# Hybrid decoder trunk: when transposing transfers are issued, how their data are taken over, and one head that turns its values on PE

## The chip, the cores and the metric

One core of one Trainium2 chip. The metric is device time in microseconds (us): the time of one execution, here the median of three runs. Besides the timed runs one execution was profiled; its trace gives the start and length of each instruction on the engines PE (TensorE), ACT (ScalarE), DVE (VectorE), POOL (GpSimd) and SP (SyncE, which issues most transfers).

## The reference

512 tokens of width 1024 get 16 learned meta tokens put ahead of them (528 in all), pass two layers and a final norm, and the meta tokens are dropped. Everything is float32.

```python
h = concat([meta, x])                        # 528 x 1024
h = h + gla_branch(rmsnorm(h), ...)          # 4 heads, value width 512 each
h = h + diff_branch(rmsnorm(h), ...)         # 8 heads, value width 256 each
out = rmsnorm(h[16:], g_final)
```

The first layer is gated linear attention: per head it projects queries, keys, values and a gate, weighs score blocks of 128 x 128 tokens with a decay, multiplies them with the values, norms each row over the head's width, multiplies with the gate and projects back. The second layer is differential softmax attention: per head two score matrices of 528 x 528 with a position bias, `a = softmax1 - lam * softmax2`, `a @ v`, the same norm, gate and projection back.

## The kernel before, in words

**Precision.** Each float32 operand of a product is split into a high and a low part (`split`, L259: ACT copies to the high part, DVE subtracts to get the low one), and a product is three matmuls (high x high, high x low, low x high). So each weight block that comes in costs one ACT and one DVE instruction before PE can use it.

**Projections.** A projection of 256 output columns is a `Unit` (L384): seven products of 12 matmuls (`product`, L376) on sums and differences of the operand blocks. Its results come out in two planes of 128 channels x 528 tokens; when a plane is done, `tail(1)` (L442) and at the very end `tail(0)` (L461) are called. ACT moves partial results (L400), DVE adds them (L425, L427).

**Values must be turned.** Projections give channels on the partitions, and the value product needs tokens there. In the first head of each layer and in the very last head PE turns them: `to_tokens` (L796) makes four transposes of 128 x 128 (L801) and a short one for the meta tokens (L802) into two small banks, and `split` and `split3` (L350) take them over. `post` does this 2.4 us of filler after the plane is complete (L830). All other heads turn by transfers (`turn_by_dma`, L528): ACT copies a plane into two planes of 16-bit halves (L539) and writes them to DRAM (`vd`, L540); SP's transposing transfers bring them back with tokens on the partitions (L548, and the short `lands` for the meta tokens, L550); then `landed` (L521) takes the whole 128 x 1024 block over: ACT scales it to the high part by a constant `tick` (L523), DVE makes the low part (L525), and `split3` makes `vm`, the meta tokens' values (L355, L356, L360). `tick` is a small DVE memset (L554) tied behind the latest DVE addition (`W.mark`), so that ACT cannot take the block over before that place in DVE's order.

**Order of the work.** PE's instructions stay in program order. Those of ACT, DVE and SP are put in an order ahead of time, by program order as priority and by what is expected to be ready; functions marked `urgent` (L251) go 100 places ahead. During the run each engine works its list off in that order and waits in front of an instruction whose inputs are not there. Transposing transfers of L548 are kept in program order on SP.

Filler work (units, output projections) is a queue of generators in a `Weaver` (L74). `fill(us)` runs the next ones for so many us by their own count (a product counts 0.33 for three matmuls); the steps of a head (scores, value products, rows) are called between fills. `defer` and `follow` are clocks that run on this count: after both planes of a value unit have left, `follow` starts the transfers 8.0 us later and the takeover 10.0 us after that (L543). `W.land()` forces what is still out: in the first layer ahead of the blocks of a head (L1250), in the second at the start of a head (L1712).

**Weights.** `Weights` (L151) has a list of jobs and keeps two of them loaded (`fetch`, L166): when all parts of a job are split, it is dropped and the next but one is asked for, by `load` (L282), 1 MB into one of two `raw` buffers. A job enters the list when its unit is queued. In the second layer a head's queue is [output product of the pair before, in heads 2, 4 and 6], gate unit, value unit of the next head, key unit, query projection (L1716 to L1728; head 6 has another order); the next head's jobs enter only at that head's start (L1707).

**The second layer's steps.** L1738: A (scores), B (turn), C (values, `L348` on `v` and then L1587 on `vm`), E (rows) on blocks 3 to 0; step 4 of the list is C on block 3, the head's first value product. The filler is shared out by weights 1.5, 1.1, 1.1, 0.5 (L1741) with 3.0 us ahead of the first (L1744) and 3.0 held back (22.0 in head 6). The queue's length by its own count is 37.6 us a head (8.9 + 9.2 + 9.2 + 10.3), 60 with an output product (22.4).

**The first layer's heads.** From the value unit of head 1 on: values, output projection of the head before (heads 1 and 2 only), two gate units, landing, then the blocks (`gla_blocks`, L1140), whose first needs `vm` (L1152). In the last head the output projection of the head before comes after the landing, as the blocks' filler (L902 and L910).

Of the kernel before, what the change touches and what calls it, by code (L numbers as in the profile page):

```python
# [11 lines left out]
F32 = mybir.dt.float32  # L12
# [8 lines left out]
P = 128  # L21
# [52 lines left out]
class Weaver:  # L74


    def __init__(self):
        self.queue, self.late, self.left, self.stop = deque(), [], 0.0, None
        self.away = []

    def add(self, gen, us=0.0):
        self.queue.append(gen)
# [23 lines left out]

    def land(self):

        while self.away:
            self.onward(1000.0)  # L110

    def spent(self, us):
        self.onward(us)
# [37 lines left out]
class Weights:  # L151
# [44 lines left out]
    def done(self, p):  # L196
        self.room[p.kind] += 1
        self.pump()
# [8 lines left out]
def trunk(ctx, tc, x, meta, g_norm, gla_w_in, gla_w_gate_up, gla_b_gate, gla_gnorm, gla_w_out,  # L207
# [21 lines left out]
    def T(p, shape, dt, tag, **kw):  # L229
        uid[0] += 1  # L230
        return p.tile(shape, dt, tag=tag, name=f"{tag}_{uid[0]}", **kw)
# [36 lines left out]
    def load_w(w, r0, nk, c0):  # L268
        ncol = 2048 // nk
        t = T(wp, [P, nk, ncol], F32, "raw")  # L270
        sp.dma_start(t, w[r0:r0 + nk * P, c0:c0 + ncol].rearrange("(k p) c -> p k c", p=P))
        return t

    def load_blocks(w, c0):

        t = T(wp, [P, 4, 512], F32, "raw")
        for i in range(2):
            sp.dma_start(t[:, 2 * i:2 * i + 2, :].rearrange("p j (k c) -> p (j k) c", k=4),
                         w[:, c0 + i * P:c0 + (i + 1) * P].rearrange("(k p) c -> p k c", p=P))
        return t  # L280

    def load(key):  # L282
        return load_w(*key) if len(key) == 4 else load_blocks(*key)

    def w_pair(shape):
        return [T(wp, shape, F32R, tag) for tag in ("wh", "wl")]
# [4 lines left out]
        split(wh, wl, raw[:, :, ca:ca + ncol])  # L291
        return wh, wl

    W = Weaver()
    ws = Weights(lambda *key: load(key), {"pair": 2, "sum": 1, "a11": 1, "a12": 1, "a22": 1})

    def halves_of(c):
# [52 lines left out]
    def split3(dst, src, lo, scale=None):  # L350


        kw = {} if scale is None else {"scale": scale}
        hi = dst[:32].bitcast(F32)
        act.activation(dst[:32], src, AF.Copy, **kw)  # L355
        act.activation(dst[96 - lo:128 - lo], src, AF.Copy, **kw)  # L356
        if scale is None:
            dve.tensor_tensor(dst[lo:lo + 32], src, hi, op=ALU.subtract)
        else:
            dve.scalar_tensor_tensor(dst[lo:lo + 32], src, scale, hi, op0=ALU.mult, op1=ALU.subtract)  # L360
# [156 lines left out]
    def words(t):  # L517

        return t.bitcast(U16)

    def landed(hi, lo, src, one, rest):  # L521

        a = act.activation(hi, src, AF.Copy, scale=one)  # L523
        with tc.issue_after(a.ins):
            dve.tensor_tensor(lo, src, hi.bitcast(F32), op=ALU.subtract)  # L525
            rest()

    def turn_by_dma(planes, groups, ends, us, done):  # L528

        n = planes.shape[2]  # L530
        vd = T(dp, [2, P, 2, n], U16, "vd", bufs=3)
        rows = vd.rearrange("m p h c -> (m p h) c")
        raw = planes.rearrange("p m c -> p (m c)")[:, :2 * NR].rearrange("p (b c) -> p b c", c=2 * P)
        left, lands = [0, 1], []

        @urgent
        def leave(m, src):
            pl = words(planes[:, m, :]).rearrange("p (h c) -> p h c", h=2)
            act.activation(pl, words(src).rearrange("p (c h) -> p h c", h=2), AF.Copy)  # L539
            act.dma_start(vd[m], pl)  # L540
            left.remove(m)
            if not left:
                W.follow((8.0, turn), (us, land))  # L543

        def turn():
            for blocks, c0 in groups:
                o = words(raw[:, blocks, :])
                tc.keep_in_program_order(sp.dma_start(o, rows[:, c0:c0 + P * o.shape[1]], transpose=True))  # L548
            lands.append(T(mp, [P, 1, 2 * P], F32, "lands"))
            sp.dma_start(words(lands[0]), rows[:, ends:ends + P], transpose=True)  # L550

        def land():
            tick = T(mp, [P, 1], F32, "tick", bufs=2)
            tc.add_manual_dep(dve.memset(tick, 1.0).ins, W.mark.ins.name, mybir.DependencyInfo(  # L554
                mybir.DependencyClass.NoSync, mybir.DependencyReason.DATA), reason="place")
            done(raw, lands[0][:32, 0, :], tick)

        return leave

# [261 lines left out]
    def q_gla_v(hd, s):  # L821
        us = [want_unit(g_w_in, 2048 + 512 * hd + c) for c in (0, 256)] if hd else v_first

        def turned_back(m, vt):
            def post():
                pt, pm = to_tokens(vt, BLK, vt[:, :32])
                cs = slice(m * P, (m + 1) * P)
                split(s.v[0][:, :, cs], s.v[1][:, :, cs], pt.rearrange("p (b c) -> p b c", b=4))
                split3(s.vm[:, cs], pm, 32, short[:, NM:NM + 1])
            W.defer(2.4, post)  # L830

        def turner(h):
            def done(pt, pm, one):
                cs = slice(256 * h, 256 * h + 256)
                landed(s.v[0][:, :, cs], s.v[1][:, :, cs], pt, one, lambda: split3(s.vm[:, cs], pm, 32, short[:, NM:NM + 1]))
            return turn_by_dma(b_all[:, 2 * h:2 * h + 2, :], [(slice(0, 4), NM)], 0, 10.0, done)

        gens = []
        for h, u in enumerate(us):
            vts = []  # L840

            def dst(h=h, vts=vts):
                if h == 0:
                    s.vm = T(gp, [M3, 512], F32R, "vm0")
                    s.v = [T(gp, [P, 4, 512], F32R, f"v{i}") for i in range(2)]
                vts.extend([tmp(), tmp()])
                return vts

            if hd:
                gens.append(W.add(Unit(u, X, 1.0, dst, lambda i, vts=vts, leave=turner(h): leave(i, vts[i]))))  # L850
            else:
                def evac(i, banks, h=h, vts=vts, dst=dst):
                    if i == 0:
                        dst()
                    for n, bank in enumerate(banks):
                        act.activation(vts[i][:, n * HT:(n + 1) * HT], bank[:, :HT], AF.Copy)
                    turned_back(2 * h + i, vts[i])

                gens.append(W.add(plain_unit(u, evac)))
        return gens[0]  # L860
# [593 lines left out]
    def turned_back2(s, m, vt, first=False):  # L1454
        if not first:

            urgent(dve.tensor_copy)(vt[:, HT:HT + 8], vt[:, 2 * HT:2 * HT + 8])

        @urgent
        def post():  # L1460
            end = L if first else 272
            pt, pm = to_tokens(vt, RBLK if first else HBLK, vt[:, end - 32:end])
            cs = slice(m * P, (m + 1) * P)
            split3(s.vm[:, cs], pm, 32, short[:, NM + 1:NM + 2])
            split(s.v[0][:, :, cs], s.v[1][:, :, cs], pt.rearrange("p (b c) -> p b c", b=4))

        def done(pt, pm, one):
            landed(s.v[0], s.v[1], pt, one, lambda: split3(s.vm, pm, 32, short[:, NM + 1:NM + 2]))

        if first or s is heads[-1]:  # L1470
            W.defer(2.2 if first else 1.4, post)
        else:
            if m:
                s.leave = turn_by_dma(T(ep, [P, 2, 536], F32, "planes", bufs=1),
                                      [(slice(3, 1, -1), 0), (slice(1, None, -1), 272)], 240, 10.0, done)
            s.leave(m, vt[:, :536])

    def q_diff_z(hd, s):
# [228 lines left out]
    for hd in range(D_HEADS):  # L1707
# [1 line left out]
        s = heads[hd]  # L1709
        W.finish(projs[hd])  # L1710
        W.settle()
        W.land()  # L1712
        s.scored = False
        out2 = None
        keep = {D_HEADS - 1: 0.0, D_HEADS - 2: 22.0}.get(hd, 3.0)
# [29 lines left out]
        for n, (f, b) in enumerate(steps):  # L1745
            if last and n == 4:
                if values[hd] in W.queue:
                    W.finish(values[hd])
                W.settle()
                W.fill(2.0)  # L1750
            if n == 5 and gates[hd] in W.queue:
                W.finish(gates[hd])
            if last and n == 5:
                gfin = T(xp, [P, D], F32, "x0", bufs=1)
                sp.dma_start(gfin, g_final.partition_broadcast(P))
            if n == 5:
                if out2 in W.queue:
                    W.finish(out2)
                ys.append([yt[:, hd % 2, i] for i in range(2)])
            f(b)  # L1760
            if f is A and b == 0:
                s.scored, W.stop = True, None
                if not last:
                    heads[hd + 1].T = bias_tile(hd + 1)
            W.fill(max((W.left - keep) * share[f] / sum(share[g] for g, _ in steps[n:]),
                       (4.0 if hd % 2 == 0 else 3.0) if n == len(steps) - 2 else 2.4 if f is C else 0.0))
# [56 lines left out]
```

## Time and profile before

| | |
|---|---|
| median of 3 runs | 1008.28 us (1008.08 to 1010.28) |
| the profiled execution | 1010.31 us |
| its span, first to last instruction | 1008.5 us |
| PE's mean granted clock | 0.99 of full |
| value planes written for turning | 24 (12 from `keep`, first layer; 12 from `planes`, second) |
| transposing issues on SP | 30 (6 `keep`, 12 `planes`, 12 `lands`) |
| weight loads of the second layer on SP | 42 halves of 512 KB, landing after 5.5 us (median) |

Rows of a timeline are: start us, length us, engine, line, operation, output <- input, tile, count, and in brackets the engine's idle time before it and what ended it. An engine name with q (SPq, ACTq) is that engine's issue of a transfer, not the transfer. Rows with a count are merged, and their length runs from the first to the end of the last. Rows of stages are: from:to, length, busy time (and count) of PE, PEld (weight loads into the array), DVE, ACT, POOL, then PE's granted clock, the share in which the DMA engines were busy, and GB/s. Groups of a tile have least/median/greatest length in ns. Rows of waits have the total, the number and the longest, in us.

### The profile page before, as it was taken

How to read it: one execution, taken by the hardware profiler on the slowest of the kernel's cores; microseconds unless marked ns; L12 is line 12 of the kernel's file. 1: busy time of each engine (PE TensorE's matmuls, PEld its weight loads, DVE VectorE, ACT ScalarE, POOL GpSimd, SP SyncE). 2: the span in 40 equal slices, each digit the busy share in tenths (PEclk: the TensorE clock that was granted, in tenths of full speed). 3: DMA queues.
4: the chain of work that ended last, by engine and by line, in shares of the span. 5: the costliest groups of instructions: out<-in, count | busy, mean ns of one | idle time of the engine just before them, and what ended most of it. 6: DMA issues, size and time to landing. Idle time of an engine off the chain costs nothing. (4 is left out here: it accounts for less than half of the span.)

```text
span 1008.5 us, 18098 instructions
## 1 busy us (share of the span) xinstructions
PE 975.0 (97%) x7023; PEld 916.6 (91%) x7023; DVE 778.7 (77%) x1574; ACT 614.6 (61%) x1292; POOL 51.5 (5%) x68
## 2 busy tenths in 40 slices
PE   8999999999999999899999899999999999999997
PEld 7999999899999999799899799898998999988896
DVE  7888885877778787456998696886967879676785
ACT  6775855475546666536667476466774666654584
POOL 1000000001000100000000101001010010100001
PEclk8999999999999999899999999999999999999999
DMA  7212324541363336122232424335251362623212
GB/s 192 81 50 79 88 84 134 100 114 44 111 152 84 84 105 152 50 84 80 86 97 72 114 84 142 84 96 132 58 169 45 98 153 61 160 65 95 84 64 83
DMA packets 156296, 98.63 MB, mean 98 GB/s; under 512 B 38429, under 2 KB 142141, under 8 KB 156208
## 3 DMA queue, kind: packets, MB, share of 16 engines
q1 hardware_dynamic: 152752, 90.92, 33.7%
q10 hardware_dynamic: 3456, 6.54, 1.9%
q8 instruction: 55, 0.90, 0.4%
q14 instruction: 33, 0.27, 0.1%
HBM read 83.64 MB, written 8.66 MB: 92 GB/s over the span
## 5 line engine op out<-in xcount | busy, mean ns | idle before, releaser
L263 DVE TENSOR_TENSOR wl<-raw,wh 128x1024 fp32r<-128x1024 f32 x99 | 120.7, 1221 | 24.1 <-ACT wh L262 21.1
L262 ACT ACTIVATE wh<-raw 128x1024 fp32r<-128x1024 f32 x99 | 104.1, 1053 | 48.2 <-PE by L902 20.2
L379 PE MATMUL bx<-x,wh 128*128 128x264 f32 (+1 forms) x640 | 95.8, 287 | 3.4 <-ACT u L400 2.5
L379 PE MATMUL bv<-x,wh 128*128 128x264 f32 (+1 forms) x656 | 97.1, 286 | 0.2 <-DVE t L425 0.2
L379 PEld LDWEIGHTS bx<-x,wh 128*128 128x128 f32 x640 | 84.5, 188 | 5.4 <-ACT u L400 3.6
L379 PEld LDWEIGHTS bv<-x,wh 128*128 128x128 f32 x656 | 86.3, 189 | 0.9 <-DVE t L425 0.6
L263 DVE TENSOR_TENSOR wl<-sum,wh 128x1024 fp32r<-128x1024 f32 x41 | 50.1, 1222 | 19.9 <-ACT wh L262 17.7
L369 PE MATMUL bx<-x,wh 128*128 128x512 f32 (+1 forms) x256 | 63.6, 391 | 0.0
L400 ACT ACTIVATE u<-bx 128x264 f32<-128x264 f32 (+1 forms) x120 | 45.3, 378 | 27.6 <-PE bx L379 25.8
L1558 ACT ACTIVATE p<-p,st 128x528 f32<-128x528 f32 (+3 forms) x64 | 36.4, 569 | 42.1 <-DVE st L1556 41.9
L1594 POOL TENSOR_TENSOR st<-st,mhalf 128x1 f32<-128x1 f32 x32 | 31.4, 982 | 475.3 <-ACT on L1592 407.0
L379 PE MATMUL bv<-x,wl 128*128 128x264 f32 (+1 forms) x328 | 55.2, 285 | 0.0
L262 ACT ACTIVATE wh<-sum 128x1024 fp32r<-128x1024 f32 x41 | 43.2, 1053 | 19.6 <-issue 10.3
L379 PE MATMUL bx<-x,wl 128*128 128x264 f32 (+1 forms) x320 | 53.7, 285 | 0.0
L369 PEld LDWEIGHTS bx<-x,wh 128*128 128x128 f32 x256 | 45.4, 192 | 8.2
L379 PE MATMUL by<-x,a12h 128*128 128x264 f32 (+1 forms) x320 | 46.7, 285 | 0.0
L379 PE MATMUL bx<-x,a11h 128*128 128x264 f32 (+1 forms) x320 | 46.2, 285 | 0.0
L262 ACT ACTIVATE a11h<-raw 128x512 fp32r<-128x512 f32 x41 | 25.7, 627 | 33.2 <-DMA raw<-in_diff_w_in_dram 19.1
L379 PEld LDWEIGHTS bv<-x,wl 128*128 128x128 f32 x328 | 45.9, 188 | 0.0
L379 PEld LDWEIGHTS bx<-x,wl 128*128 128x128 f32 x320 | 45.0, 188 | 0.6 <-DVE wl L263 0.5
L379 PEld LDWEIGHTS bx<-x,a11h 128*128 128x128 f32 x320 | 42.2, 188 | 0.8
L379 PEld LDWEIGHTS by<-x,a12h 128*128 128x128 f32 x320 | 41.7, 188 | 0.5 <-DVE t L425 0.5
(475 smaller groups left out, 2640.7 us busy)
## 6 DMA issues: line engine op xcount, KB each, us to landing
raw<-in_gla_w_in_dram SPq DMA_DIRECT2D x48, 512.0 KB, 4.8
raw<-in_diff_w_in_dram SPq DMA_DIRECT2D x42, 512.0 KB, 5.5
raw<-in_diff_w_in_dram SPq DMA_DIRECT2D x11, 1024.0 KB, 5.8
raw<-in_gla_w_out_dram SPq DMA_DIRECT2D x8, 1024.0 KB, 5.4
raw<-in_diff_w_out_dram SPq DMA_DIRECT2D x8, 1024.0 KB
vd<-planes ACTq DMA_DIRECT2D x12, 268.0 KB, 3.1
vd<-keep ACTq DMA_DIRECT2D x12, 264.0 KB, 2.4
T<-bdr SPq DMA_DIRECT2D x8, 264.0 KB, 3.8
```

The lines of the kernel that those rows point to most:

```text
L262: act.activation(hi, src, AF.Copy)
L263: dve.tensor_tensor(lo, src, hi.bitcast(F32), op=ALU.subtract)
L369: pe.matmul(bank, a[:, k, :], b[k] if n0 is None else b[k][:, n0 + i * nn:n0 + (i + 1) * nn], start=n == 0 and ks[0] == 0, stop=n == len(t ...
L379: pe.matmul(bank[:, :x[q].shape[2]], w[p][:, k * P:(k + 1) * P], x[q][:, k, :], start=first and i == 0, stop=i == len(PASSES) - 1, skip_gr ...
L400: act.activation(t, self.bx[:, :self.n], AF.Copy, scale=self.sc)
L1558: act.activation(p[:, :nk], p[:, :nk], AF.Exp, scale=-1.0, bias=st[:, m:m + 1], accum_out=st[:, 2 + m:3 + m])
L1594: pool.tensor_tensor(ms, ms, mhalf[:, :1], op=ALU.pow)
```

## The change

Four things:

- When both planes have left, the transfers wait 4.0 us of filler and then in a list `behind`; the next call of `load` empties it right after its own issue. `land` empties it as well. The short transfer is now kept in program order too.
- The takeover is in pieces: 11.0 us of filler after the issue `tick` is set, 1.5 later the first 128 of the 256 channels are taken over, 2.5 later the other 128, 1.5 later `vm`, tied behind ACT's latest piece.
- In the second layer landing is forced ahead of step 4 of a head (its first value product), no longer at the head's start.
- In the first layer's last head both value units turn on PE, by `turned_back`, as head 0's do.

```diff
-        self.away = []
+        self.away, self.behind = [], []
...
     def land(self):
-        while self.away:
+        while self.away or self.behind:
             self.onward(1000.0)
+            while self.behind:
+                self.behind.pop(0)()
...
     def load(key):
-        return load_w(*key) if len(key) == 4 else load_blocks(*key)
+        t = load_w(*key) if len(key) == 4 else load_blocks(*key)
+        while behind:
+            behind.pop(0)()
+        return t
...
-    def landed(hi, lo, src, one, rest):
-        a = act.activation(hi, src, AF.Copy, scale=one)
-        with tc.issue_after(a.ins):
-            dve.tensor_tensor(lo, src, hi.bitcast(F32), op=ALU.subtract)
-            rest()
+    def landed(hi, lo, src, one):
+        W.split = act.activation(hi, src, AF.Copy, scale=one)
+        dve.tensor_tensor(lo, src, hi.bitcast(F32), op=ALU.subtract)
...
             if not left:
-                W.follow((8.0, turn), (us, land))
+                W.follow((4.0, lambda: behind.append(turn)))
...
-            sp.dma_start(words(lands[0]), rows[:, ends:ends + P], transpose=True)
+            tc.keep_in_program_order(sp.dma_start(words(lands[0]), rows[:, ends:ends + P], transpose=True))
+            W.follow((us, place), (1.5, lambda: done(raw[:, :, :P], tick[0], 0)), (2.5, lambda: done(raw[:, :, P:], tick[0], 1)),
+                     (1.5, rest))
+        def rest():
+            with tc.issue_after(W.split.ins):
+                last(lands[0][:32, 0, :])
...
-            return turn_by_dma(b_all[:, 2 * h:2 * h + 2, :], [(slice(0, 4), NM)], 0, 10.0, done)
+            return turn_by_dma(b_all[:, 2 * h:2 * h + 2, :], [(slice(0, 4), NM)], 0, 11.0, done, last)
...
-                gens.append(W.add(Unit(u, X, 1.0, dst, lambda i, vts=vts, leave=turner(h): leave(i, vts[i]))))
+                leave = turner(h) if hd < G_HEADS - 1 else lambda i, vt, h=h: turned_back(2 * h + i, vt)
+                gens.append(W.add(Unit(u, X, 1.0, dst, lambda i, vts=vts, leave=leave: leave(i, vts[i]))))
...
         W.settle()
-        W.land()
         s.scored = False
...
                 W.fill(2.0)
+            if n == 4:
+                W.land()
```

More of the change, by code (lines that the diff above doesn't have):

```diff
@@ L280, in load_blocks @@
         return t
+    W = Weaver()
+    behind = W.behind
     def load(key):
-        return load_w(*key) if len(key) == 4 else load_blocks(*key)
+        t = load_w(*key) if len(key) == 4 else load_blocks(*key)
+        while behind:
+            behind.pop(0)()
+        return t
     def w_pair(shape):
@@ L292, in split_w @@
         return wh, wl
-    W = Weaver()
     ws = Weights(lambda *key: load(key), {"pair": 2, "sum": 1, "a11": 1, "a12": 1, "a22": 1})
@@ L519, in words, with turn_by_dma @@
         return t.bitcast(U16)
-    def landed(hi, lo, src, one, rest):
-        a = act.activation(hi, src, AF.Copy, scale=one)
-        with tc.issue_after(a.ins):
-            dve.tensor_tensor(lo, src, hi.bitcast(F32), op=ALU.subtract)
-            rest()
-    def turn_by_dma(planes, groups, ends, us, done):
+    def landed(hi, lo, src, one):
+        W.split = act.activation(hi, src, AF.Copy, scale=one)
+        dve.tensor_tensor(lo, src, hi.bitcast(F32), op=ALU.subtract)
+    def turn_by_dma(planes, groups, ends, us, done, last):
         n = planes.shape[2]
@@ L549, in turn, with place @@
             lands.append(T(mp, [P, 1, 2 * P], F32, "lands"))
[L550 to L554, printed above, removed]
+            tc.keep_in_program_order(sp.dma_start(words(lands[0]), rows[:, ends:ends + P], transpose=True))
+            W.follow((us, place), (1.5, lambda: done(raw[:, :, :P], tick[0], 0)), (2.5, lambda: done(raw[:, :, P:], tick[0], 1)),
+                     (1.5, rest))
+        tick = []
+        def rest():
+            with tc.issue_after(W.split.ins):
+                last(lands[0][:32, 0, :])
+        def place():
+            tick.append(T(mp, [P, 1], F32, "tick", bufs=2))
+            tc.add_manual_dep(dve.memset(tick[0], 1.0).ins, W.mark.ins.name, mybir.DependencyInfo(
                 mybir.DependencyClass.NoSync, mybir.DependencyReason.DATA), reason="place")
-            done(raw, lands[0][:32, 0, :], tick)
         return leave
@@ L832, in turner, with done, last @@
         def turner(h):
-            def done(pt, pm, one):
-                cs = slice(256 * h, 256 * h + 256)
-                landed(s.v[0][:, :, cs], s.v[1][:, :, cs], pt, one, lambda: split3(s.vm[:, cs], pm, 32, short[:, NM:NM + 1]))
-            return turn_by_dma(b_all[:, 2 * h:2 * h + 2, :], [(slice(0, 4), NM)], 0, 10.0, done)
+            def done(pt, one, m):
+                cs = slice(256 * h + m * P, 256 * h + m * P + P)
+                landed(s.v[0][:, :, cs], s.v[1][:, :, cs], pt, one)
+            def last(pm):
+                split3(s.vm[:, 256 * h:256 * h + 256], pm, 32, short[:, NM:NM + 1])
+            return turn_by_dma(b_all[:, 2 * h:2 * h + 2, :], [(slice(0, 4), NM)], 0, 11.0, done, last)
         gens = []
@@ L1465, in post, with done, last @@
             split(s.v[0][:, :, cs], s.v[1][:, :, cs], pt.rearrange("p (b c) -> p b c", b=4))
-        def done(pt, pm, one):
-            landed(s.v[0], s.v[1], pt, one, lambda: split3(s.vm, pm, 32, short[:, NM + 1:NM + 2]))
+        def done(pt, one, m):
+            landed(s.v[0][:, :, m * P:m * P + P], s.v[1][:, :, m * P:m * P + P], pt, one)
+        def last(pm):
+            split3(s.vm, pm, 32, short[:, NM + 1:NM + 2])
         if first or s is heads[-1]:
@@ L1474, in turned_back2 @@
                 s.leave = turn_by_dma(T(ep, [P, 2, 536], F32, "planes", bufs=1),
-                                      [(slice(3, 1, -1), 0), (slice(1, None, -1), 272)], 240, 10.0, done)
+                                      [(slice(3, 1, -1), 0), (slice(1, None, -1), 272)], 240, 11.0, done, last)
             s.leave(m, vt[:, :536])
```

## The prediction

> **What bounds it.** I read the page's head first, then the list of PE's waits, then PE's timeline, whose rows have the idle time before them in brackets with what ended it, and last the stages around the long ones.
>
> ```profile
> span 1008.5 us, 18098 instructions
> PE 975.0 (97%) x7023; PEld 916.6 (91%) x7023; DVE 778.7 (77%) x1574; ACT 614.6 (61%) x1292; POOL 51.5 (5%) x68
> ```
> ```profile
> 187.22 0.39 PE L902 MATMUL bv<-y,wh 128*128 128x264 f32 x1 [2.18 <-DVE hT L910]
> 292.52 0.39 PE L902 MATMUL bv<-y,wh 128*128 128x264 f32 x1 [1.76 <-DVE hT L910]
> 410.05 0.59 PE L1152 MATMUL ps<-vm,am 96*16 96x512 f32 x1 [4.63 <-DVE vm L360]
> 571.50 0.44 PE L1601 MATMUL ps<-ident,on 128*128 128x128 f32 x2 [4.38 <-ACT on L1595]
> ```
> PE is the bound: 975.0 of 1008.5 us, so 33.5 us idle in all. Four waits hold 13.0 of them, and all four stand beside a transposing transfer or its takeover. The two long ones cost more than themselves:
>
> ```profile
> 187.00:195.00 8.00, 7.78 (x62) 7.62 (x63) 6.30 (x13) 3.01 (x4) 0.00 (x0) 1.00 0.57 145
> 410.00:416.00 6.00, 5.95 (x29) 5.71 (x29) 0.91 (x3) 1.35 (x3) 0.54 (x1) 0.55 0.17 65
> 572.00:577.00 5.00, 5.00 (x18) 4.12 (x17) 4.94 (x9) 3.00 (x8) 0.55 (x1) 0.66 0.39 105
> ```
> In these stage rows the third figure from the end is PE's granted clock. It is 0.55 for 6 us behind the 4.63 us wait, a loss of 0.45 x 6 = 2.7 us, and 0.66 for 5 us behind the 4.38 us wait, a loss of 1.7 us; behind the 2.18 us wait it is 1.00.
>
> **Step 1: the first layer's last head turns on PE.** In that head the second value unit leaves by ACT, is turned by SP's transfers, and is taken over in one lump just when PE wants `vm`:
>
> ```profile
> 386.45 0.34 ACTq L540 DMA_DIRECT2D vd<-keep  x1
> ...
> 397.77 1.15 SPq L550 DMA_TRANSPOSE lands<-vd  x1
> ...
> 406.38 1.13 ACT L523 ACTIVATE v<-keep,tick 128x1024 fp32r<-128x1024 f32 x1
> ...
> 409.42 0.47 DVE L360 SCALAR_TENSOR_TENSOR vm<-lands,short,vm 32x256 fp32r<-32x256 f32 x1
> ```
> Values leave at 386.5 and are ready at 409.9; the other heads have an output projection in between, this one has only its gates, and landing is forced at the first block. With PE turning, each of the four planes is taken 2.4 us of filler after it is complete, so by about 391. The wait and its slow clock go: 4.63 + 2.7 = 7.3 us. Added on PE are four times four transposes and one short one, as in the last head now:
>
> ```profile
> 965.42 0.44 PE ps L801 x4
> 965.86 0.11 PE ps L802
> ```
> That is 4 x 0.55 = 2.2 us, all on the path, since PE has no idle time there to hide it. ACT and DVE:
>
> ```profile
> L262 ACT ACTIVATE v<-ps x8: 577/598/614, 39.9 to 965.9; 128x512 fp32r<-128x512 f32 x8
> L263 DVE TENSOR_TENSOR v<-ps,v x8: 665/682/692, 40.9 to 966.7; 128x512 fp32r<-128x512 f32 x8
> L539 ACT ACTIVATE keep<-t x12: 1067/1084/1086, 153.7 to 385.4; 128x1056 uint16<-128x1056 uint16 x12
> ```
> ACT loses four plane copies of 1.08, DVE gains 4 x 0.68 for 2 x 1.22. The first unit's share falls at 372 to 378, where DVE has no gap and the cross scores wait on it; a block holds two of the four small banks. I bound this at 0 to 1.5 us (two of DVE's 0.68 us on the path) and take 0.5, just under one of them. What is late next is that head's gate; between the first block's output and its rows lie two stretches of filler, so I count nothing for it. Step 1: -7.3 + 2.2 + 0.5 = **-4.6 us**, between -5.1 and -3. The head also drops four writes, two big and two small transposing transfers; SP then fetches output weights earlier, which nobody waits for.
>
> **Step 2: transfers behind a weight load.** The 4.38 us wait goes back to a blocked SP queue:
>
> ```profile
> 551.50 0.34 SPq L1423 DMA_DIRECT2D T<-bdr  x1
> ...
> 554.17 2.36 DVE L263 TENSOR_TENSOR wl<-raw,wh 128x1024 fp32r<-128x1024 f32 x2 [0.40 <-ACT wh L262]
> ...
> 556.15 2.59 SPq L548 DMA_TRANSPOSE planes<-vd  x2
> ...
> 558.79 1.25 SPq L550 DMA_TRANSPOSE lands<-vd  x1
> ...
> 560.14 22.69 SPq L278 DMA_DIRECT2D raw<-in_diff_w_in_dram  x6
> ...
> 564.78 0.63 ACT L262 ACTIVATE a11h<-raw 128x512 fp32r<-128x512 f32 x1 [6.03 <-DMA raw<-in_diff_w_in_dram]
> ```
> The weight buffer is free when DVE has read it, at 556.5 at the latest; the load goes at 560.14, behind three transposing issues of 2.59 + 1.25 us. ACT stands 6.03 us in front of a split whose data are not there, and in its queue behind it are two key splits, a weight split and the normalization whose result (L1595) PE waits for. With the load in front it can go 3.6 us earlier; the wait shrinks from 4.38 to 0.8 us, which by the 2.18 us row brings no slow clock. That gives -3.6 - 1.7 = **-5.3 us**. The bounds are 0, if ACT's split is placed as much earlier as the load, and -6.1, if all goes. The transfers themselves come later by one load's issue (about 1 us), and nothing waits for them for 20 us.
>
> The Trainium skill, page "Advanced Engine Details and Errata", section "X-Bar Transpose (TRN2)", says that transposing transfers are as fast as regular ones. By that they would hold SP only 3 x 0.34 us as the 551.50 load does, and the sum of this step would be -1.0; the rows with 2.59 for two and 1.25 for one disagree.
>
> **Step 3: pieces in the first layer's heads 1 and 2.** Before the 2.18 us wait DVE is a backlog:
>
> ```profile
> 172.90 1.20 SPq L278 DMA_DIRECT2D raw<-in_gla_w_in_dram  x2
> 174.14 6.13 SPq L548 DMA_TRANSPOSE keep<-vd  x1
> ...
> 180.55 0.69 DVE L318 TENSOR_TENSOR sum<-raw 128x512 f32<-128x512 f32 x1 [1.65 <-DMA raw<-in_gla_w_in_dram]
> ...
> 183.65 1.22 DVE L525 TENSOR_TENSOR v<-keep,v 128x1024 fp32r<-128x1024 f32 x1
> ...
> 185.60 1.23 DVE L263 TENSOR_TENSOR wl<-raw,wh 128x1024 fp32r<-128x1024 f32 x1 [0.23 <-ACT wh L262]
> ...
> 187.09 0.42 DVE L910 TENSOR_TENSOR hT<-hT,by 128x264 f32<-128x264 f32 x1
> ```
> The sums start late because their load shares the rings with two transposing groups, and the takeover (1.22, then 0.47 of `vm`) stands ahead of the additions that free PE's banks. Load first and halves of 0.6 and 0.7 us with 2.5 us of PE work between them loosen both; the work itself grows by two fixed costs of some 0.1 us each. Of 2.18 + 1.76 = 3.9 us I take **-2.5**, nearer to all than to nothing, because either cause alone covers most of it; the bounds are -3.9 and +2, the latter a wait as long as today's at another bank.
>
> **Step 4: later landing in the second layer.** Here I expect a cost. From the end of a head's value unit to the next head no weight load is left in the program's order (the key and query weights are already asked for), so the transfers are written down at the next head's first load, and the 11 + 1.5 + 2.5 + 1.5 = 16.5 us count from there. Landing is forced ahead of step 4, the first value product. In heads 2 and 4 the output product of the pair before lies in the filler, which I work out as 21 us: all has landed. In heads 1, 3 and 5 it does not:
>
> ```profile
> 580.29:599.61 19.32, 16.20 (x129) 15.75 (x128) 1.00 0.20 56
> ```
> This row holds the filler's matmuls alone (L379) from head 1's start to its first value product: 129, or 43 yields of 0.33 = 14.2 us. The first half is taken at 12.5; the second half and `vm` are forced, at the very place where PE wants them:
>
> ```profile
> 599.62 1.59 PE L348 MATMUL ps<-v,aT 128*128 128x256 f32 x12
> ...
> 599.81 0.62 ACT L262 ACTIVATE a12h<-raw 128x512 fp32r<-128x512 f32 x1
> 600.33 1.05 ACT L262 ACTIVATE wh<-sum 128x1024 fp32r<-128x1024 f32 x1
> ```
> ```profile
> 728.29 1.57 PE L348 MATMUL ps<-v,aT 128*128 128x256 f32 x12
> 728.32 0.62 ACT L262 ACTIVATE a12h<-raw 128x512 fp32r<-128x512 f32 x1
> ```
> ```profile
> 855.19 1.59 PE L348 MATMUL ps<-v,aT 128*128 128x256 f32 x12
> 855.87 0.62 ACT L262 ACTIVATE a12h<-raw 128x512 fp32r<-128x512 f32 x1
> ```
> A half costs 0.60 on ACT and 0.68 on DVE (rows of step 1). Behind both weight splits that is 601.4 + 1.3 = 602.7, a wait of 3.0 us in head 1. In heads 3 and 5 one such split is ahead: 728.9 + 1.3 is 1.9 us late, 856.5 + 1.3 is 2.6 us late; 7.5 in all. The order on ACT and DVE is not the program's, though: what is ready may go into an earlier gap, and from `place` on both halves are ready, 4 us before. So the bounds are 0 and +7.5 us, and I take the middle, **+4**. Head 6 holds work back and also gets some 14 us, but its filler is an output product without gates to compute, so I count nothing there. At the heads' starts the lump's work goes away, beside a PE that hardly waits there today; I take 0.
>
> **Sum.** -4.6 - 5.3 - 2.5 + 4 = -8.4 us. The profiled execution took 1010.31 us with a span of 1008.5; the median of the runs is 1008.28, and I take the difference off that: 999.9, say **1000 us**. About 0.2%, 2 us, can be told from no change.
>
> **Rivals.** (a) *Everything lands for nothing.* The halves of step 4 slip into gaps and the first layer's waits go whole: -5.1 - 6.1 - 3.9 = -15, so 993. For it speaks that ACT is 61% busy; against it DVE where head 1 would need it, 5.00 of 5 us busy (the columns after the length are PE, its weight loads, DVE, ACT):
>
> ```profile
> 597.00:602.00 5.00, 5.00 (x43) 5.00 (x43) 5.00 (x15) 4.59 (x12) 0.00 (x0) 1.00 0.29 69
> ```
> Chance 0.12.
>
> (b) *The load gains nothing.* ACT's split of 564.78 was put there by an order made ahead of time; if the load moves 3.6 us, that order may move with it, and ACT stands before the data as now. Then -4.6 - 2.5 + 4 = -3, so 1005. The skill's rule above would end nearly here, at 1004. For it speaks how often that split waits in the second layer (us, times, longest):
>
> ```profile
> ACT a11h L262 <- DMA raw<-in_diff_w_in_dram: 19.1, 5, 6.0
> ```
> Four more such waits share 13.1 us and none of them shows as a long one of PE. Chance 0.20, a bit over half of it beyond 0.2%.
>
> (c) *Slower: the forced landing becomes the long wait.* If second half and `vm` come behind further splits in heads 1, 3 and 5, each wait passes the length that slows the clock, and each costs what the one at 571.5 does: 4.4 + 1.7 = 6.1, or 18.3 us against gains of 12.4. That is 1014, and 1020 if head 6 joins. It decides from 4.1 us a head on. For it speaks the busy DVE; against it the 1.9 to 3.0 us above. Chance 0.18.
>
> On the clock, the Trainium skill ("TensorE: Matmul & The Clock Gate", "Part 1: The HAM clock gate") puts the limit at an idle window of about 3.4 us. Our rows allow anything between 2.18 and 4.38; by the page, waits of 3.0 us would stay free of it, and the worst of step 4 without slow clock is 1003.
>
> The forecast itself has 0.50, with a range of its own from 996 to 1004. The whole range is 992 to 1010: it takes in (a), (b) and the mild end of (c). Faster by over 0.2%: 0.50 + 0.12 + 0.11 = 0.73; within: 0.08 of (b) and 0.02 of (c), 0.10; slower: 0.17.
>
> **What would show it.** Step 1: 16 more turns on L801, six `keep` transfers on SP become four, no wait on L1152 near 405 and clock 1.00 behind it. Step 2: the load near 556.6 ahead of L548, ACT's wait there under 3 us. Step 3: the two L902 waits under 1 us. Step 4: waits of L348 `ps<-v,aT` on DVE `v` at the first value product of heads 1, 3 and 5 and none in 2 and 4. I am wrong if such waits pass 4 us, or if as long a wait as today's turns up elsewhere because the whole order on ACT and DVE is made anew.

## The result and the profile after

| | before | changed |
|---|---|---|
| median, both kernels on the same chip | 1009.07 us (11 runs, 1005.76 to 1012.21) | 1007.97 us (11 runs, 1006.29 to 1011.45) |
| ratio, 95% interval | | 0.9997 [0.998, 1.0014] |
| profiled execution, its span | 1010.31, 1008.5 us | 1006.47, 1004.7 us |

The change makes no difference that can be measured. The prediction was 1000 us, with a chance of 0.73 for faster; it was wrong. The time lies inside its whole range of 992 to 1010 us, but the gain of 8 us that it forecast did not come. The head of the changed kernel's page shows an equally full PE:

```profile
span 1004.7 us, 18151 instructions
...
PE 975.7 (97%) x7043; PEld 920.2 (92%) x7043; DVE 780.0 (78%) x1586; ACT 615.0 (61%) x1304; POOL 49.6 (5%) x68
```

All four long waits of before are gone, and three pairs of new ones have come. PE's timeline of the changed kernel has them at the first value product (now L355) of heads 1, 3 and 5 of the second layer:

```profile
583.95 0.38 PE L355 MATMUL ps<-v,aT 128*128 128x256 f32 x1 [2.92 <-ACT v L530]
585.11 2.43 PE L355 MATMUL ps<-v,aT 128*128 128x256 f32 x11 [0.78 <-DVE v L531]
...
716.49 0.58 PE L355 MATMUL ps<-v,aT 128*128 128x256 f32 x1 [3.26 <-ACT v L530]
717.65 2.72 PE L355 MATMUL ps<-v,aT 128*128 128x256 f32 x11 [0.58 <-DVE v L531]
...
849.51 0.58 PE L355 MATMUL ps<-v,aT 128*128 128x256 f32 x1 [3.96 <-ACT v L530]
850.68 2.71 PE L355 MATMUL ps<-v,aT 128*128 128x256 f32 x11 [0.58 <-DVE v L531]
```

That is 3.70 + 3.84 + 4.54 = 12.1 us. To see what a step is worth, take the start of one PE instruction in both traces and see how far the changed kernel leads there. Its `vm` products in the value steps (L1587 before, L1606 now) lead by 12.5 us at the layer's start (543.04 against 530.53) and by 17.5 behind head 0 (573.18 against 555.71). Then the lead melts: the last one starts at 993.00 and 989.14, 3.9 us apart. The loss lies in three stretches. The stage rows go from the last such product of the head before to the first of heads 1, 3 and 5 (length, then busy PE, its weight loads, DVE, ACT, POOL, then the granted clock); first before, then the changed kernel:

```profile
573.18:601.05 27.87, 27.87 (x199) 26.47 (x198) 26.45 (x62) 19.84 (x44) 0.55 (x1) 0.95 0.19 49
697.30:729.70 32.40, 30.52 (x212) 27.98 (x211) 29.30 (x67) 21.08 (x47) 2.57 (x1) 1.00 0.26 71
826.25:856.62 30.37, 29.95 (x208) 27.80 (x207) 28.86 (x66) 21.29 (x48) 0.70 (x1) 1.00 0.29 78
```
```profile
555.71:587.34 31.63, 27.93 (x200) 26.40 (x199) 28.02 (x64) 20.58 (x45) 0.55 (x1) 0.97 0.30 86
684.30:720.16 35.86, 31.76 (x211) 29.14 (x210) 30.58 (x69) 21.20 (x47) 2.58 (x1) 0.93 0.32 91
817.13:853.19 36.06, 31.52 (x209) 29.07 (x207) 31.81 (x72) 21.93 (x49) 0.70 (x1) 0.93 0.34 95
```

The same matmuls take 3.8, 3.5 and 5.7 us longer, 12.9 in all. Read two things here. PE's idle time in the second set is 3.7 + 4.1 + 4.5 = 12.3 us, against 2.3 in the first, and the clock of 0.93 adds to it. And DVE works 28.0 of 31.6 us, 30.6 of 35.9 and 31.8 of 36.1. Where the values are wanted it has no gap at all: these stage rows of the changed kernel end just as the late takeover begins or runs, and DVE (the third busy time) is idle for 0.10 us in each:

```profile
571.00:584.00 13.00, 10.08 (x85) 9.86 (x83) 12.90 (x34) 11.63 (x26) 0.00 (x0) 1.00 0.19 51
706.00:717.00 11.00, 7.74 (x62) 7.29 (x60) 10.90 (x29) 9.30 (x21) 0.00 (x0) 0.92 0.25 76
838.00:850.00 12.00, 8.04 (x65) 7.62 (x63) 11.90 (x32) 10.33 (x25) 0.00 (x0) 0.93 0.23 65
```

Why the values are late is seen in head 1. DVE's timeline of the changed kernel ahead of the late product:

```profile
576.78 0.42 DVE L434 TENSOR_TENSOR t<-bv,u 128x256 f32<-128x256 f32 x1
...
580.88 0.42 DVE L434 TENSOR_TENSOR t<-by,u 128x264 f32<-128x264 f32 x1
...
581.94 0.50 DVE L1582 SCALAR_TENSOR_TENSOR p<-p,st,p 128x272 f32<-128x272 f32 x1
...
582.43 0.69 DVE L265 TENSOR_TENSOR a12l<-raw,a12h 128x512 fp32r<-128x512 f32 x1
582.46 0.06 DVE L567 MEMSET tick<- 128x1 f32 x1
...
583.77 1.29 DVE L531 TENSOR_TENSOR v<-planes,v 128x512 fp32r<-128x512 f32 x2
585.09 0.47 DVE L367 SCALAR_TENSOR_TENSOR vm<-lands,short,vm 32x256 fp32r<-32x256 f32 x1
```

and ACT's of the same time:

```profile
580.94 1.06 ACT L264 ACTIVATE wh<-sum 128x1024 fp32r<-128x1024 f32 x1
582.56 1.33 ACT L530 ACTIVATE v<-planes,tick 128x512 fp32r<-128x512 f32 x2 [0.56 <-DVE tick L567]
```

PE wants the values at 583.95 - 2.92 = 581.03. The gate `tick`, which the halves need, is tied by the program behind the addition at 576.78 (the latest one written down before it), but it runs on DVE only at 582.46, behind a weight split; then both halves come in one lump (x2). The data themselves had been there for over 25 us: their transfers went out at 544 to 550, and the planes land at most 4.2 us after a transfer's issue. SP's timeline shows them, with the weight load now in front:

```profile
542.92 0.99 SPq L280 DMA_DIRECT2D raw<-in_diff_w_in_dram  x2
544.01 4.65 SPq L553 DMA_TRANSPOSE planes<-vd  x2
548.72 1.25 SPq L555 DMA_TRANSPOSE lands<-vd  x1
```

### The profile page after: what moved, and what is told of

The parts are those of the page before. It is cut to its first block, busy times and chain, and to the rows that moved or that the text cites. A ratio compares the mean times of both kernels' runs of the same rounds, so it can differ in the third digit from the quotient of the medians.

```text
span 1004.7 us, 18151 instructions
## 1 busy us (share of the span) xinstructions
PE 975.7 (97%) x7043; PEld 920.2 (92%) x7043; DVE 780.0 (78%) x1586; ACT 615.0 (61%) x1304; POOL 49.6 (5%) x68
## 5 line engine op out<-in xcount | busy, mean ns | idle before, releaser
L386 PE MATMUL bv<-x,wh 128*128 128x264 f32 (+1 forms) x656 | 98.3, 288 | 0.0
L386 PE MATMUL bx<-x,wh 128*128 128x264 f32 (+1 forms) x640 | 95.7, 287 | 1.2 <-ACT u L407 1.1
L386 PEld LDWEIGHTS bv<-x,wh 128*128 128x128 f32 x656 | 87.4, 191 | 0.4
L386 PEld LDWEIGHTS bx<-x,wh 128*128 128x128 f32 x640 | 85.2, 190 | 2.4 <-ACT u L407 1.6
L407 ACT ACTIVATE u<-bx 128x264 f32<-128x264 f32 (+1 forms) x120 | 45.4, 379 | 30.8 <-PE bx L386 28.6
L1577 ACT ACTIVATE p<-p,st 128x528 f32<-128x528 f32 (+3 forms) x64 | 36.4, 569 | 33.8 <-DVE st L1575 33.5
L386 PE MATMUL bv<-x,wl 128*128 128x264 f32 (+1 forms) x328 | 55.9, 288 | 0.0
L386 PE MATMUL bx<-x,wl 128*128 128x264 f32 (+1 forms) x320 | 53.5, 285 | 0.0
L264 ACT ACTIVATE wh<-sum 128x1024 fp32r<-128x1024 f32 x41 | 43.2, 1055 | 12.1 <-PE bv L386 4.4
L355 PE MATMUL ps<-v,aT 128*128 128x256 f32 x240 | 38.6, 304 | 12.2 <-ACT v L530 10.1
L355 PEld LDWEIGHTS ps<-v,aT 128*128 128x128 f32 x240 | 34.8, 206 | 15.0 <-ACT v L530 10.8
L386 PEld LDWEIGHTS bv<-x,wl 128*128 128x128 f32 x328 | 46.8, 192 | 0.0
L386 PE MATMUL by<-x,a12h 128*128 128x264 f32 (+1 forms) x320 | 46.5, 285 | 0.0
L386 PE MATMUL bx<-x,a11h 128*128 128x264 f32 (+1 forms) x320 | 46.2, 285 | 0.0
L386 PEld LDWEIGHTS bx<-x,wl 128*128 128x128 f32 x320 | 44.9, 188 | 0.4 <-DVE wl L265 0.2
```

Source lines behind the costliest of these rows:

```text
L264: act.activation(hi, src, AF.Copy)
L355: pe.matmul(ps, l, r, start=first and n == 0, stop=last and n == 2, **kw)
L386: pe.matmul(bank[:, :x[q].shape[2]], w[p][:, k * P:(k + 1) * P], x[q][:, k, :], start=first and i == 0, stop=i == len(PASSES) - 1, skip_gr ...
L407: act.activation(t, self.bx[:, :self.n], AF.Copy, scale=self.sc)
L1577: act.activation(p[:, :nk], p[:, :nk], AF.Exp, scale=-1.0, bias=st[:, m:m + 1], accum_out=st[:, 2 + m:3 + m])
```

## The experiments

The theory after the result: the first three steps brought what was forecast or more, and the later landing in heads 1, 3 and 5 gave nearly all of it back, because the gate and the halves stand in full queues of DVE and ACT. The rivals: the new order on ACT and DVE costs in many places; the forced landing alone is at fault; the gate alone is. Times are medians, ratios are to the kernel before on the same chip (1008.8 to 1010.3 us).

### One part alone, or one part undone

**The second layer's count.** One number, and with it the landing comes 6 us of filler earlier:

```diff
-    [(slice(3, 1, -1), 0), (slice(1, None, -1), 272)], 240, 11.0, done, last)
+    [(slice(3, 1, -1), 0), (slice(1, None, -1), 272)], 240, 5.0, done, last)
```

> The changed kernel with the count from issue to takeover in the second layer cut from 11.0 to 5.0 us, so that halves and meta part are out by 10.5 us of filler and nothing is forced at the first value product. Theory (the three waits of heads 1, 3 and 5 and the slow clock behind them, 12.1 + 3.6 us in the trace of the changed kernel, come from the takeover's place alone): no wait of PE for v at the first value products, 993 us, 15 below the changed kernel. Rival (DVE is full in those heads, and whatever is taken over there delays something): the waits move to scores or partial results, 1003 us or more.

Measured: **988.51 us, ratio 0.9803 [0.9778, 0.9828]**. This version beats both kernels, and by more than the 993 us expected. DVE takes the values over some 12 us ahead of the product:

```profile
564.96 0.06 DVE L567 MEMSET tick<- 128x1 f32 x1
...
567.42 0.69 DVE L531 TENSOR_TENSOR v<-planes,v 128x512 fp32r<-128x512 f32 x1
...
568.55 0.47 DVE L367 SCALAR_TENSOR_TENSOR vm<-lands,short,vm 32x256 fp32r<-32x256 f32 x1
```

The product starts at 580.74 with no wait, and the three stretches are these:

```profile
555.54:582.17 26.63, 26.63 (x200) 25.48 (x198) 25.89 (x60) 20.00 (x45) 0.55 (x1) 1.00 0.24 66
678.86:708.86 30.00, 29.92 (x211) 27.80 (x210) 27.86 (x64) 21.25 (x47) 2.58 (x1) 1.00 0.27 74
805.08:835.64 30.56, 30.06 (x209) 27.88 (x208) 29.84 (x69) 21.89 (x50) 0.70 (x1) 1.00 0.30 78
```

87.2 us against 103.6 with count 11 and 90.6 before: the loss was in the landing's time, not in the first three steps nor spread over the kernel. DVE is just as full there, 25.9 of 26.6 us in head 1; only the order in its queue is another. And the landing now costs less than the old one did: the three stretches are 3.4 us shorter than before.

**The last head of the first layer alone.** The kernel before with that head's values turned on PE, nothing else:

```diff
-    gens.append(W.add(Unit(u, X, 1.0, dst, lambda i, vts=vts, leave=turner(h): leave(i, vts[i]))))
+    leave = turner(h) if hd < G_HEADS - 1 else lambda i, vt, h=h: turned_back(2 * h + i, vt)
+    gens.append(W.add(Unit(u, X, 1.0, dst, lambda i, vts=vts, leave=leave: leave(i, vts[i]))))
```

> The kernel before with the last head of the first layer turned on PE and nothing else. Theory (5.8 us won in that head in the trace of the changed kernel): 5 to 6 us below the kernel before, 1003.5 us, the wait of L1152 gone and clock 1.00 behind it. Rival (the gain of that head needs the pieces and the load order of the heads before): 2 us or less.

Measured: 1003.7 us against 1009.42, ratio 0.9953 [0.9936, 0.9971], 5.7 us less. From the end of head 2's blocks to that of head 3's it takes 77.04 us (350.07 to 427.11), as in the changed kernel (344.28 to 421.29, 77.01), against 82.82 before. The other long waits stay, slightly moved:

```profile
185.86 0.39 PE L903 MATMUL bv<-y,wh 128*128 128x264 f32 x1 [2.19 <-DVE hT L911]
...
563.95 0.48 PE L1602 MATMUL ps<-ident,on 128*128 128x128 f32 x1 [3.52 <-ACT on L1596]
```

**The first layer's parts alone.** The changed kernel with the second layer's turning, takeover and landing as before:

```diff
-    s.leave = turn_by_dma(..., 240, 11.0, done, last)
+    s.leave = turn_by_dma0(..., 240, 10.0, done)
...
         W.settle()
+        W.land()
...
-            if n == 4:
-                W.land()
```

> The changed kernel with the second layer's turning as before (transfers 8.0 us after the planes, takeover in one lump 10.0 us later or at the head's start, so no wait at the first value products). Theory (the first layer's parts win 12.5 us and the second layer's lose them): 12 to 13 us below the kernel before, 996.5 us, with a wait of some 4 us for L1595 still in head 0 of the second layer. Rival (the first layer's lead is lost again whatever the second layer does, because its order is made anew): within 4 us of the kernel before.

Measured: 1000.0 us, ratio 0.9914 [0.9889, 0.9939]; by the profiled spans 997.1 against 1008.5. The gain is a little smaller than expected by the medians (9.4), nearer to it by the spans (11.4). Undoing only the second layer makes the changed kernel 8 us faster. The wait at the blocked SP queue is back:

```profile
558.22 0.69 PE L1656 MATMUL ps<-ident,on 128*128 128x128 f32 x2 [3.95 <-ACT on L1650]
```

### Gate, place or count

**The gate marked urgent.** `@urgent` on `place`, count 11 kept.

> The changed kernel with one edit: the small memset that opens the takeover goes 100 places ahead in DVE's order. Theory (it was emitted 4 us before the value product but stood behind DVE's backlog, at 582.46 where 576 was expected): it runs within 1 us of its place, both halves follow in gaps of ACT, the waits in heads 1, 3 and 5 fall to 0 to 1.5 us each without slow clock, 995 to 999 us. Rival (what counts is that the second half and the meta part are forced at the value product): the memset is early, but waits of 2 to 3 us a head stay, 1001 to 1004 us.

Measured: 1004.23 us, ratio 0.9951 [0.9931, 0.997]. The gate runs at 576.39 instead of 582.46, but ACT's halves only at 579.62 and DVE's at 581.66; waits of 0.73 + 1.61, 1.08 + 1.62 and 1.88 + 1.70 us stay. The time is at the rival's end, and its waits of 2.3 to 3.6 us a head are there: the gate is a part of the cause, not the whole. The run also shows where the tie is: the gate now starts right behind the addition that stood at 576.78 (here 576.01).

**Gate, halves and `vm` all urgent.**

```diff
-    W.follow((us, place), (1.5, lambda: done(raw[:, :, :P], tick[0], 0)), (2.5, lambda: done(raw[:, :, P:], tick[0], 1)),
-             (1.5, rest))
+    W.follow((us, urgent(place)), (1.5, lambda: urgent(done)(raw[:, :, :P], tick[0], 0)),
+             (2.5, lambda: urgent(done)(raw[:, :, P:], tick[0], 1)), (1.5, urgent(rest)))
```

> The changed kernel, count 11 kept, with the gate, both halves and vm all marked to go ahead of other waiting work on their engines (in e2 the gate alone, 1004.2 us). Theory (the second layer loses because the takeover stands in the queues of VectorE and ScalarE behind work that has time; count 5 helps only by getting ahead of it): the waits at the first value product of heads 1, 3 and 5 fall below 1.5 us each, 988 to 994 us. Rival (it is the place in the program's order: half and vm are written down at step 4 and can't be had before PE asks for them): waits of 2 us and more stay in each of the three heads, 999 to 1005 us.

Measured: 999.39 us, ratio 0.9917 [0.9886, 0.9948]: the time falls in the rival's range, at its lower end, and the waits of 1.7, 2.0 and 2.7 us a head lie between the two. The longest pair is in head 5:

```profile
840.17 0.58 PE L355 MATMUL ps<-v,aT 128*128 128x256 f32 x1 [1.89 <-ACT v L530]
841.58 2.71 PE L355 MATMUL ps<-v,aT 128*128 128x256 f32 x11 [0.83 <-DVE v L531]
```

So both hold: going ahead in the queues wins back about 8.6 us of the 19.5 that count 5 does, and the rest needs the takeover to be written down earlier, which also moves the addition behind which the gate is tied.

**Count 8, count 6.5 and count 2.** The same number as in the first experiment.

> The changed kernel with the second layer's count at 8 instead of 11 (5 gave 988.5 us). By count nothing is forced then: 8 + 1.5 + 2.5 + 1.5 = 13.5 us of the 14.2 us of filler. Theory (what decides is where the gate and the halves stand in the queues of VectorE and ScalarE, 2 to 6 us behind the place where the program writes them down): PE still waits at the first value product of heads 1, 3 and 5, 1 to 3 us each, so 992 to 998 us. Rival (only the forced landing costs; whoever is taken over by count before step 4 is in time): no wait of PE over 1 us there, 987 to 990 us.

Measured with 8: 1005.38 us, ratio 0.9973 [0.9956, 0.9989], slower than the theory's 992 to 998, and with its waits. By count nothing is forced here, yet the second half is late. By the kernel's own due times it is now written down behind step 3, the third block of scores, whose functions are marked urgent. ACT takes it right behind that block's exponentials (L1577), DVE 2.6 us later, and PE waits (ACT's, DVE's and PE's timeline):

```profile
582.89 0.51 ACT L1577 ACTIVATE p<-p,st 128x272 f32<-128x272 f32 x1
583.30 0.19 ACT L1577 ACTIVATION_READ_ACCUMULATOR p<-p,st 128x1 f32 x1
583.39 0.71 ACT L530 ACTIVATE v<-planes,tick 128x512 fp32r<-128x512 f32 x1
```
```profile
586.03 0.68 DVE L531 TENSOR_TENSOR v<-planes,v 128x512 fp32r<-128x512 f32 x1
```
```profile
584.15 0.39 PE L355 MATMUL ps<-v,aT 128*128 128x256 f32 x1 [0.53 <-ACT v L530]
586.77 0.50 PE L355 MATMUL ps<-v,aT 128*128 128x256 f32 x2 [2.23 <-DVE v L531]
```

> Count 6.5, between 5 (988.5 us) and 8 (1005.4 us). Theory (the cost rises step by step, as each instruction falls behind one more piece of other work on VectorE or ScalarE): 990 to 1000 us, with waits of 0.5 to 2 us in some of the three heads. Rival (all or nothing: either the second half lands ahead of the last weight split of the stretch or behind it): within 3 us of one of the two ends.

Measured with 6.5: 988.51 us, ratio 0.9799 [0.9777, 0.9821], the same as with 5. The theory of a slow rise falls: it is all or nothing. With 6.5 the second half is written down ahead of step 3, by the same due times, and the trace has gate, halves and `vm` at 565.05 to 569.1. Between 6.5 and 8 lie 17 us of the kernel's time.

Which of two things makes the jump is not shown. By the same due times the gate's tie moves as well: with 6.5 the gate stands behind an addition at 564.08 and runs at 565.05, with 8 behind one at 575.05 and runs at 575.42. And a place behind step 3 is not late by itself: with 6.5 `vm` is written down behind it too, and DVE still takes it over at 568.65.

> The second layer's count at 2 instead of 11. Theory (at 5 there is slack already: no PE wait over 1.1 us is left): the same as with 5, 987 to 990 us. Rival (the earlier takeover meets other work of VectorE at the head's start, or data not yet there, and gives part of it back): 991 to 996 us with new waits at the heads' starts.

Measured with 2: 992.64 us, ratio 0.9856 [0.9835, 0.9876], above the theory's range and in the rival's, though its runs (990.88 to 996.79) overlap those of count 5 (987.4 to 993.15). No wait stands at the value products, but PE waits 1.69 us at 820.70 and 1.49 at 909.14 for ACT to empty a bank (L407): an early takeover seems to be in somebody's way too.

### What the first layer and the load needed

**One lump**, on top of count 5: gate, halves and `vm` at once, in both layers.

```diff
-    W.follow((us, place), (1.5, ...), (2.5, ...), (1.5, rest))
+    W.follow((us, lump))
...
+        def lump():
+            place()
+            done(raw[:, :, :P], tick[0], 0)
+            done(raw[:, :, P:], tick[0], 1)
+            rest()
```

> Count 5 in the second layer (988.5 us) and the landed parts taken over in one lump, gate, both halves and vm at once, in both layers; the order behind a weight load stays. Theory (the prediction's step 3: load first alone covers most of what heads 1 and 2 of the first layer won, and the second layer lands so early that a lump meets no PE wait): 988.5 to 990.5 us, the hT waits of heads 1 and 2 under 1 us. Rival (pieces are what won the 6.2 us there): the hT waits of 2.2 and 1.8 us are back, with some more, 992.5 to 995 us.

Measured: 991.08 us, ratio 0.9823 [0.9805, 0.9841], just above the theory's range; the runs (988.72 to 993.2) overlap those of count 5. The first layer's heads keep their gain: from head 0's first block to the end of head 2's blocks it is 109.25 to 343.53, 234.3 us, against 234.0 in the changed kernel and 240.3 before. By the two traces what is lost against count 5 stands in head 6, at a wait of 2.43 us (L386, for ACT to empty a bank) that is 1.08 us with pieces.

**No load in front**, on top of count 5:

```diff
-                W.follow((4.0, lambda: behind.append(turn)))
+                W.follow((4.0, turn))
```

The transfers go out 4.0 us of filler after the planes here; in the kernel before it was 8.0.

> Count 5 in the second layer (988.5 us) and pieces, but the transposing transfers go out by count alone as before, not behind a weight load. Theory (a blocked SP queue made the 4.4 us wait ahead of L1620's matmul and its slow clock, 5.0 us between the two traces): that wait is back with 3 to 4.5 us, 992 to 996 us. Rival (the wait went because the order on ScalarE was made anew, not because of SP): no wait over 2 us there, 987 to 990 us.

Measured: 1001.3 us, ratio 0.9924 [0.9904, 0.9943], more than the theory's 992 to 996. SP's queue is blocked as before, and PE waits as before:

```profile
545.05 2.61 SPq L553 DMA_TRANSPOSE planes<-vd  x2
547.71 1.25 SPq L555 DMA_TRANSPOSE lands<-vd  x1
549.06 9.68 SPq L280 DMA_DIRECT2D raw<-in_diff_w_in_dram  x4
```
```profile
559.90 0.69 PE L1620 MATMUL ps<-ident,on 128*128 128x128 f32 x2 [4.11 <-ACT on L1614]
```

From `vm` product to `vm` product around that wait it takes 11.2 us (551.10 to 562.31), with the load in front 5.8 (549.73 to 555.54): 5.4 us. Another 3.5 lie around a wait of 3.03 at 919.87, the rest in smaller ones. The first layer here takes 110.64 to 345.47, 234.8 us: it keeps its gain without the load in front as well. What the runs with one lump and with no load have in common, the 4.0 us in place of 8.0 and the short transfer in program order, was not undone alone.

## Why the prediction was wrong, point by point

Each step by how far the lead grew in the two traces:

| step | forecast | measured | from |
|---|---|---|---|
| 1, last head on PE | -4.6 (-5.1 to -3) | -5.8 | 82.82 to 77.01 us; alone 5.7 |
| 2, load in front | -5.3 (-6.1 to 0) | -4.9 | 562.42 to 573.18 before, 549.89 to 555.71 now |
| 3, pieces, heads 1 and 2 | -2.5 (-3.9 to +2) | -6.2 | 240.26 to 234.01 us |
| 4, later landing | +4 (0 to +7.5) | +12.9, with smaller places +13.6 | three stretches; 17.5 to 3.9 of lead |

**Step 4 failed.** The prediction found the place, the heads (1, 3 and 5 and none of 2, 4, 6) and by its count the pieces left over at the forced landing. What failed is the sentence "what is ready may go into an earlier gap, and from `place` on both halves are ready, 4 us before", with which it halved its own 7.5 us, and 7.5 as the end of the range. There is no gap between that place and the product: DVE is busy for 12.90 of 13.00 us there in head 1. The prediction's own row in rival (a), DVE 5.00 of 5 us busy, said so of the kernel before. And `place` is no point in time but one more instruction in DVE's queue: free from the addition at 576.78 on, it stood behind scores, weight sums and weight splits until 582.46 and ran 1.4 us after PE wanted the values (1.8 and 2.5 us in heads 3 and 5). The waits worked out without gaps were 3.0, 1.9 and 2.6 us; they came as 3.7, 3.8 and 4.5. ACT stood 0.56, 1.55 and 1.55 us before the gate, and the first half, which the prediction had counted as taken, came behind the gate as well. The bound also left out the clock, which the prediction had priced only in rival (c):

```profile
716.00:722.00 6.00, 4.93 (x21) 4.64 (x22) 2.07 (x4) 2.69 (x7) 0.55 (x1) 0.50 0.29 100
849.00:855.00 6.00, 4.91 (x21) 4.61 (x22) 2.10 (x4) 2.02 (x6) 0.55 (x1) 0.50 0.30 103
```

This is rival (c) in its kind and in its heads; it was priced there at 18.3 us and cost 12.9. The time stayed near 1008 and not at 1014 because of that, and because the gains of steps 1 to 3 came to 16.9 us in place of 12.4. That gains and loss cancel so nearly is chance.

**Step 3 was sized too small.** The prediction gave less than the two waits it quoted, 3.9 us, and made them its bound. By the stage rows of these heads (110.72 to 350.98 before, 110.27 to 344.28 now) PE's idle time fell from 4.7 to 0.4 us, small waits included, and its busy time by 1.9 us with the same matmuls, at a clock of 1.00 in both; what that is was not settled. That either cause alone covers most of it agrees with the runs: with one lump, or with no load in front, the gain stays within 0.8 us. It is not shown, since a third cause that both runs share would do the same.

**Steps 1 and 2 were right**, 1 a little beyond its bound: from 350.98 to 433.80 before and 344.28 to 421.29 now, PE's idle time fell from 6.4 to 1.3 us, which is more than the one wait of 4.63 us that was counted. Rival (b) fell: the order on ACT moved with the load, and ACT's wait for the data there is 0.93 us. Rival (a)'s 993 was possible in this code, but not with 11 and not with 8; with 6.5 or 5 the time is below it.

## What to carry to other kernels

A gate instruction has a place in its engine's queue, and whatever it releases cannot be earlier than that; "ready from here on" needs a look at what stands in front of it. Before you count on a gap, look for it in the stretch from the gate to the use, not in a mean over the head: with count 5 DVE was 25.9 of 26.6 us busy and the takeover still found its place early, with count 11 there was none left where it could go. Where you find no gap, take the worst case of the queue as the likely one and add the clock. And when a part of a change gives back what the others bring, move its place before you judge the whole: here one number made 2% of the time.

## What the runs showed of the hardware

The clock fell behind shorter waits than the 4.4 us on which the prediction built, but not behind each of them. In the lump's run the granted clock, third from the end of the stage row, was 0.56 behind a single wait of 2.43 us:

```profile
907.47 0.81 PE L386 MATMUL bx<-x,wh 128*128 128x264 f32 x2 [2.43 <-ACT u L407]
```
```profile
907.40:911.00 3.60, 3.53 (x18) 3.53 (x18) 2.89 (x7) 1.59 (x6) 0.00 (x0) 0.56 0.00 0
```

In the run with the first layer's parts alone a wait of 2.53 us at the same product left it at 1.00:

```profile
917.49 1.24 PE L386 MATMUL bx<-x,wh 128*128 128x264 f32 x8 [2.53 <-ACT u L407]
```
```profile
917.40:921.00 3.60, 3.51 (x29) 3.51 (x30) 3.54 (x9) 2.18 (x8) 0.00 (x0) 1.00 0.00 0
```

So no length of wait divides the two here. With the gate urgent, 2.71 us at 919.34 brought 0.54 (919.3 to 923); with count 8, 2.23 us at 586.77 left it at 1.00 (stage 586 to 592). Nor is the sum of a pair of waits a clean limit: 0.53 + 2.23 us with 0.39 us of matmuls between left the clock at 1.00, 1.89 + 0.83 with 0.58 between brought 0.57 for 8 us (840 to 848, all urgent). The Trainium skill, page "TensorE: Matmul & The Clock Gate", section "Part 1: The HAM clock gate", puts the fall behind at least one idle window of about 3.4 us; the 2.43 us here do not agree, and the measurement decides.

The Trainium skill, page "Advanced Engine Details and Errata", section "X-Bar Transpose (TRN2)", has transposing transfers as fast as regular ones. The prediction read that as the time for which their issue holds SP, which the page does not say. With no load in front, their issue held SP for 2.61 + 1.25 us, and that order cost 5.4 us in head 0; no run here compares the speed of the transfers themselves.
